# A decoder layer in float32: h's first quads in SP's queue, k tiles 8 and 9 by sevens in the tenth gate/up group, silu's product behind a split

## The chip, the cores and the metric

The kernel runs on one core of one Trainium2 chip. The metric is the device time of one launch in microseconds, the median of several runs. The core has TensorE (PE, with its weight loads as PEld), VectorE (DVE), ScalarE (ACT), GpSimd (POOL) and SyncE (SP). SP and POOL issue the DMAs here.

## What is computed

One decoder layer on 256 tokens of width 2048, in float32: a half-step SwiGLU FFN with LayerNorm, a token mixer (multi-head latent attention beside differential attention, merged by gates), a LayerNorm, and a second half-step FFN with LayerNorm. The change lies in the two FFNs:

```python
def _swiglu(x, w_gate, w_up, w_down):
    return (jax.nn.silu(x @ w_gate) * (x @ w_up)) @ w_down      # 2048 -> 5632 -> 2048

h = _layer_norm(ALPHA * h + 0.5 * _swiglu(h, ffn1_w_gate[l], ffn1_w_up[l], ffn1_w_down[l]), ln1_g[l], ln1_b[l])
mix = _mixer(h, ...)
h = _layer_norm(ALPHA * h + mix, ln2_g[l], ln2_b[l])
h = _layer_norm(ALPHA * h + 0.5 * _swiglu(h, ffn2_w_gate[l], ...), ln3_g[l], ln3_b[l])
```

## The kernel before

**Products.** A product in float32 is made of three matmuls (`triple`, L207 to L210): each operand is split into a high part of type fp32r and the rest, and high x high, high x low and low x high are summed in PSUM. So each weight block from memory is split first (`split`, L153 to L156): ScalarE casts it (the high part, L154), VectorE subtracts (the low part, L155). The two parts go into a ring of pairs of tiles (`wring`).

**Gate and up.** In `ffn`, the weights are taken in 22 chunks of 512 columns (256 of gate, 256 of up); the first two run by `project`, the other 20 by `Hybrid.group` (L374), in ten groups p = 1 to 10 of two chunks each, over all 16 k tiles of 128. A group treats some k tiles as 2 x 2 block products by seven multiplications in place of eight ("by sevens", with the sums of activations made once by `Seven` and `Extra`, and the sums of weight blocks made in each group on VectorE, L428, or by an accumulating DMA from POOL, L430). The rest is plain. With `wide` off, k tiles 0 to 7 go by sevens (14 seven-products of two k tiles) and 8 to 15 are plain (8 units). With `wide` on, k tiles 8 and 9 go by sevens too: a third slice of one k tile in each seven-product (`eraw`, 512 columns wide), 6 plain units, and one more element in each sum of weights. Groups 2 to 9 are wide, groups 1 and 10 are not. The order of the units is a string in `group` ("15pp6p72q4q3q" when wide: digits are seven-products, p and q plain units of the two chunks).

**Order of the work.** The units are issued with a look-ahead (`look(3, 4)`): 3 units are loaded ahead, 4 more are split ahead of the products. Small jobs are put in by `later(n, fn)`, n units on. The framework then schedules the instructions of each engine by a model of its own, so that an instruction without a reason to wait may be placed far ahead of where it was written. `tc.issue_after(x)` sets an instruction behind x on x's own engine. `behind_split(n)` sets one behind the n-th newest split of the weights. `fetched[0]` is the newest plain weight block's load (L457 in a group). Weight blocks are loaded from SP (L420 those of the sevens, L457 the plain ones).

**silu.** When a bank is complete, `sum_done` (L880) and `half` (L860) evacuate it (`gus`, L885), take silu on ScalarE (`sg`, L863) and multiply by the up part on VectorE (`hb`, L869; this is `product`). Two chunks make a tile of 512 columns, which `put_h` transposes by blocks (L715) and writes to `hT` in memory (L717).

**Down.** h comes back from `hT` in quads of 4 k tiles, in two halves of 128 tokens (256 KB each): `get_h` (L890) loads a quad from POOL (L893), `split_h` (L895) splits it (tiles `h`). The down product uses quads 3, 4 and 0 first; their loads are put in with the tenth group. Most activations and weights on the way share one pool of 41 tiles (tag `act`).

Of the kernel before, what the change touches and what calls it, by code (L numbers as in the profile page):

```python
# [11 lines left out]
F32 = mybir.dt.float32  # L12
# [3 lines left out]
ALU = mybir.AluOpType  # L16
AX = mybir.AxisListType

P = 128
# [4 lines left out]
KF = DFF // P  # L24
# [35 lines left out]
def layer_kernel(ctx: ExitStack, tc: tile.TileContext, a: dict, out: bass.AP):  # L60
    nc = tc.nc
    V, S, GP, PE = nc.vector, nc.scalar, nc.gpsimd, nc.tensor
# [9 lines left out]
    def nm(s):  # L72
        uid[0] += 1
        return f"{s}_{uid[0]}"

    def act_tile(shape, dt=F32, name="act"):
        return apool.tile(shape, dt, tag="act", name=nm(name), bufs=SLOTS)

    def tmp_tile(shape, name="tmp", dt=F32):
        return small.tile(shape, dt, tag="tmp", name=nm(name), bufs=6)  # L80
# [22 lines left out]
    def later(n, fn):  # L103
        uid[0] += 1
        heapq.heappush(todo, (step[0] + n, uid[0], fn))
# [45 lines left out]
    cast, lows, fetched = [None], [None], [None]  # L151
# [192 lines left out]
    def behind_split(n):  # L344
        return tc.issue_after(line[-n].ins) if len(line) >= n else nullcontext()
# [506 lines left out]
    def ffn(n, x, wgu, wdn, residual, g, bt, each, first=None, between=None, nxt=None, cols=None, norm=None, pending=None):  # L852
        hb = {}
        hT = dram.tile([KF // 4, 2, P, 512], F32, name=f"hT{n}")

        def put_h(b, q):
            with behind_split(1):
                turn_out(hb[b, q], hT[q, b])

        def half(c, b, up, gate, wait=0):  # L860
            q = c // 2
            sg = tmp_tile([P, 256], "sg")
            S.activation(sg, gate, AF.Silu)  # L863
            if c % 2 == 0:
                hb[b, q] = tmp_tile([P, 512], "hb")
            o = (c % 2) * 256

            def product():
                V.tensor_tensor(out=hb[b, q][:, o:o + 256], in0=up, in1=sg, op=ALU.mult)  # L869
            if wait:  # L870
                later(wait, product)
            else:
                product()
            if c % 2 == 1:
                later(12, lambda: put_h(b, q))
# [4 lines left out]
        def sum_done(c, b, bank, snap, op):  # L880
            if snap is None:
                gu_done(c, b, bank)
                return
            t = tmp_tile([P, 512], "gus")
            V.tensor_tensor(out=t, in0=bank, in1=snap, op=op)  # L885
            half(c, b, t[:, 256:512], t[:, 0:256], 1)

        got, hq = {}, {}

        def get_h(q):  # L890
            raw = got[q] = act_tile([P, 2, 512], F32, "hraw")
            for b in range(2):
                nc.gpsimd.dma_start(raw[:, b, :], hT[q, b])  # L893

        def split_h(q):  # L895
            raw = got.pop(q)
            hq[q] = [act_tile([P, 2, 4, P], F32R, "h") for _ in range(2)]
            for b in range(2):
                split(*(t[:, b].rearrange("p k (i c) -> p k i c", i=4) for t in hq[q]), turned(raw[:, b, :]))
# [31 lines left out]
        for p in range(1, KF // 4):  # L931
            if p == KF // 4 - 1:
                for i, q in enumerate((3, 4, 0)):
                    later(3 + 3 * i, lambda q=q: get_h(q))
                later(13, lambda: split_h(3))
                later(16, lambda: split_h(4))
            hy.group(wgu[2 * p], wgu[2 * p + 1],
                     lambda n, b, bank, snap, op, p=p: sum_done(2 * p + n, b, bank, snap, op),
                     1 < p < KF // 4 - 1, p > 1)
        ln = LayerNorm(0.5, residual, g, bt, each, nxt, cols,  # L940
                       ((24, 26, 48, 50) if pending is None else (13, 14, 60, 62), (94, 97, 100, 103)),
                       35 if cols is None else None, pending, () if pending is None else (17, 32, 67, 82))
# [10 lines left out]
        for p in range(2):  # L953
# [16 lines left out]
            for q in range(3, KF // 4):  # L970
                first_use = min(i for i, u in enumerate(units) if len(u) == 2 and u[1] // 2 == q)
                if q in kept or (p, q) in ((0, 3), (0, 4)):
                    continue
                call(first_use - 6, lambda q=q: get_h(q))
                call(first_use, lambda q=q: split_h(q))
            if p == 0:
                for q in range(3):
                    first_use = units.index((q, 1, None))
                    if q > 0:
                        call(first_use - 6, lambda q=q: get_h(q))  # L980
                    for i, fn in enumerate(forms[q].steps(lambda q=q: got[q])):
                        call(first_use + (0, 0, 1, 2, 3)[i], fn)
                    call(first_use + 3, lambda q=q: got.pop(q))
            else:
                call(len(units) - 8, widen)
            down.run(wdn[2 * p], wdn[2 * p + 1], units, forms,
                     lambda m, b, bank, sign, p=p: ln.fold(2 * p + m, b, bank, sign),
                     lambda m, b, bank, p=p: ln.evac(2 * p + m, b, bank), calls, 8 * p)
# [407 lines left out]

    h1 = Acts(KD, "h1", (0, 1))
    ffn(1, xq, a["gu1"], a["dn1"], a["x"], a["ln1_g"], a["ln1_b"], keep(0), first_tokens, second_tokens, h1, a["ln1_cols"])

    yq = mixer(h1)  # L1400
# [3 lines left out]
    for c in range(4):  # L1404
        project(a["w_out"][c], yq, KD, 512, lambda b, bank, c=c: ln.evac(c, b, bank),
                hook=at_unit(0, widen) if c == 3 else None)
    catch_up(0)

    ffn(2, h2, a["gu2"], a["dn2"], res[1], a["ln3_g"], a["ln3_b"],
        lambda b, c, z: nc.sync.dma_start(out[b * P:(b + 1) * P, c * 512:(c + 1) * 512], z), norm=ln,  # L1410
        pending=(a["ln2_g"], a["ln2_b"]))
# [85 lines left out]
```

## Time and profile before

| | us |
|---|---|
| median of 3 runs | 1973.62 (1973.51 to 1974.14) |
| the profiled execution | 1972.85 |
| its span, first to last instruction | 1971.1 |
| TensorE busy | 1955.1 |
| VectorE busy | 1773.5 |
| ScalarE busy | 1265.5 |
| first FFN, groups 2 to 10 | 92.5 to 455.3 |
| second FFN, groups 2 to 10 | 1366.4 to 1729.1 |

Busy time counts an engine's own instructions. Matmuls overlap in the pipeline, so a mean duration of 0.39 us of a matmul of 512 columns is not its share of the time: from start to start they follow each other faster. A wait is told by its row: "[1.91 <-ACT sg L863]" means that the engine sat idle for 1.91 us and that ScalarE's instruction of line 863 ended it.

### The profile page before, as it was taken

The page shows a single profiled execution, that of the slowest core. Times are in us where ns is not written, and L with a number is a line of the kernel's source. Part 1 is how long each engine was busy: PE and PEld are TensorE (multiplying, and loading weights), DVE is VectorE, ACT ScalarE, POOL GpSimd, SP SyncE. Part 2 cuts the span into 40 slices and gives each one's busy share as a digit, 9 for nine tenths or more (in the row PEclk, how much of TensorE's full clock was granted, in tenths as well). Part 3 has the DMA queues.
Part 4 walks back from the last instruction along what each step waited for, and adds up shares of the span by engine and source line. Part 5 has one row for each costly group of instructions (what it writes and reads, how often), then busy time and mean ns, then how long its engine had stood idle before and what let it go on. Part 6 is the DMA issues. An engine that isn't in the chain of part 4 may idle for free.

```text
span 1971.1 us, 25747 instructions
## 1 busy us (share of the span) xinstructions
PE 1955.1 (99%) x8784; PEld 1620.0 (82%) x8784; DVE 1773.5 (90%) x2175; ACT 1265.5 (64%) x1650; POOL 291.0 (15%) x503
## 2 busy tenths in 40 slices
PE   9999999999999999999999999999999999999997
PEld 7888888888888898888888888888888888888886
DVE  7999999999998879988976677789999999999986
ACT  6666767676655566666667765556676776665661
POOL 0112111122100010102223120001211112210000
PEclk9999999999999999999999999999999999999999
DMA  8978888777776666767667668578888878786763
GB/s 309 287 227 262 285 270 251 235 216 281 296 235 222 209 218 254 244 224 259 223 198 241 234 216 271 199 263 254 254 263 294 243 243 249 238 321 237 274 234 124
DMA packets 147478, 485.71 MB, mean 246 GB/s; under 512 B 20961, under 2 KB 21009, under 8 KB 147345
## 3 DMA queue, kind: packets, MB, share of 16 engines
q1 hardware_dynamic: 117360, 397.99, 58.2%
q0 software_dynamic: 29984, 86.07, 16.4%
q8 instruction: 69, 1.13, 0.2%
q14 instruction: 65, 0.52, 0.1%
HBM read 455.13 MB, written 28.84 MB: 246 GB/s over the span
## 4 chain that ended last, share of the span: by engine, by line
PE 95%; DVE 2%; DMA 1%; issue 1%; ACT 0%; SPq 0%; DVEq 0%; ACTq 0%
PE mm L209 30%; PE mm L210 30%; PE mm L208 30%; DVE wring L155 1%; PE tr L208 1%; PE tr L210 1%; PE tr L209 1%; DMA sraw<-in_gu_dram 1%; PE tr L671 0%; DVE sraw L428 0%; ACT wring L154 0%; DMA raw<-in_gu_dram 0%; PE tr L1228 0%; PE tr L1301 0%; PE tr L1303 0%
## 5 line engine op out<-in xcount | busy, mean ns | idle before, releaser
L154 ACT CAST wring<-raw 128x1024 fp32r<-128x1024 f32 (+2 forms) x467 | 482.2, 1038 | 296.5 <-PE mm L210 207.2
L155 DVE TENSOR_TENSOR wring<-raw,wring 128x1024 fp32r<-128x1024 f32 (+2 forms) x467 | 559.1, 1206 | 95.4 <-ACT wring L154 92.8
L154 ACT CAST wring<-sraw 128x1024 fp32r<-128x1024 f32 x436 | 454.8, 1054 | 230.2 <-DVE sraw L428 94.2
L155 DVE TENSOR_TENSOR wring<-sraw,wring 128x1024 fp32r<-128x1024 f32 x436 | 523.2, 1228 | 21.6 <-ACT wring L154 18.8
L210 PE MATMUL mm<-wring,h 128*128 128x512 f32 (+2 forms) x1248 | 480.2, 385 | 0.0
L208 PE MATMUL mm<-wring,h 128*128 128x512 f32 (+2 forms) x1248 | 480.2, 385 | 0.0
L209 PE MATMUL mm<-wring,h 128*128 128x512 f32 (+2 forms) x1248 | 479.8, 385 | 0.0
L209 PE MATMUL mm<-wring,xs 128*128 128x512 f32 x776 | 302.2, 389 | 1.3 <-DVE wring L155 1.3
L208 PE MATMUL mm<-wring,xs 128*128 128x512 f32 x776 | 302.2, 389 | 0.0
L210 PE MATMUL mm<-wring,xs 128*128 128x512 f32 x776 | 302.0, 389 | 0.0
L209 PEld LDWEIGHTS mm<-wring,h 128*128 128x128 f32 x1248 | 234.5, 188 | 46.8 <-DVE wring L155 0.7
L210 PEld LDWEIGHTS mm<-wring,h 128*128 128x128 f32 x1248 | 234.5, 188 | 46.5 <-DVE h L155 0.7
L208 PEld LDWEIGHTS mm<-wring,h 128*128 128x128 f32 x1248 | 234.4, 188 | 46.4 <-ACT h L154 0.6
L428 DVE TENSOR_TENSOR sraw<-sraw,sraw 128x1024 f32<-128x1024 f32 x168 | 200.2, 1229 | 3.5 <-DMA sraw<-in_wdv_dram 1.6
L209 PEld LDWEIGHTS mm<-wring,xs 128*128 128x128 f32 x776 | 145.7, 188 | 32.5 <-DVE wring L155 2.3
L208 PEld LDWEIGHTS mm<-wring,xs 128*128 128x128 f32 x776 | 145.7, 188 | 30.1
L210 PEld LDWEIGHTS mm<-wring,xs 128*128 128x128 f32 x776 | 145.7, 188 | 30.0
L717 POOL DMA_DIRECT2D hT<-blocks x176 | 97.1, 562 | 370.0 <-DVE blocks L715 368.2
L208 PE MATMUL mm<-wring,x 128*128 128x512 f32 x336 | 130.8, 390 | 0.8 <-ACT wring L154 0.8
L209 PE MATMUL mm<-wring,x 128*128 128x512 f32 x336 | 131.0, 390 | 0.5 <-DVE wring L155 0.5
L210 PE MATMUL mm<-wring,x 128*128 128x512 f32 x336 | 130.6, 389 | 0.0
L430 POOL DMA_DIRECT2D sraw<-in_gu_dram x40 | 35.6, 900 | 359.4 <-DVE sraw L428 309.0
(307 smaller groups left out, 2289.6 us busy)
## 6 DMA issues: line engine op xcount, KB each, us to landing
sraw<-in_gu_dram SPq DMA_DIRECT2D x160, 512.0 KB, 5.4
raw<-in_gu_dram SPq DMA_DIRECT2D x159, 512.0 KB, 4.7
raw<-in_dn_dram SPq DMA_DIRECT2D x140, 512.0 KB, 4.7
sraw<-in_gu_dram POOLq DMA_DIRECT2D x40, 512.0 KB, 6.9
sraw<-in_dn_dram SPq DMA_DIRECT2D x36, 512.0 KB, 5.6
hraw<-hT POOLq DMA_DIRECT2D x68, 256.0 KB, 6.2
eraw<-in_gu_dram SPq DMA_DIRECT2D x64, 256.0 KB, 6.0
raw<-in_w_out_dram SPq DMA_DIRECT2D x32, 512.0 KB, 4.3
```

Source lines behind the costliest of these rows:

```text
L154: cast[0] = S.copy(hi, src)
L155: lows[0] = V.tensor_tensor(out=lo, in0=src, in1=hi.bitcast(F32), op=ALU.subtract)
L208: PE.matmul(o, xh, wh, start=first, stop=False, skip_group_check=again)
L209: PE.matmul(o, xh, wl, start=False, stop=False, skip_group_check=again)
L210: PE.matmul(o, xl, wh, start=False, stop=last, skip_group_check=again)
L428: last = V.tensor_tensor(out=R[src][i], in0=R[src][i], in1=R[add[1]][i], op=ALU.add)
L430: nc.gpsimd.dma_start(R["12"][s], source("22", s), accum_op=ALU.add)
L717: nc.gpsimd.dma_start(to.rearrange("(g r) (i f) -> i r g f", g=4, i=4)[i], t[32 * i:32 * (i + 1), :].rearrange("r (g f) -> r g f", g=4))
```

## The change

Three edits, all in `ffn`. The product that was put off by one unit (`wait`) is issued on VectorE behind the third newest weight split. The loads of h's quads 3, 4 and 0, which the tenth group puts in, are made in halves from SP (`get_half`), each behind the newest plain weight block's load, at 1, 3, 5, 7, 9 and 11 units on; before, they came whole from POOL at 3, 6 and 9. `split_h` stays at 13 and 16. And the tenth group is wide too (`p > 1` in place of `1 < p < KF // 4 - 1`; KF // 4 is 11).

```diff
             def product():
-                V.tensor_tensor(out=hb[b, q][:, o:o + 256], in0=up, in1=sg, op=ALU.mult)
+                with behind_split(3) if wait else nullcontext():
+                    V.tensor_tensor(out=hb[b, q][:, o:o + 256], in0=up, in1=sg, op=ALU.mult)
...
+        def get_half(q, b):
+            if b == 0:
+                got[q] = act_tile([P, 2, 512], F32, "hraw")
+            with tc.issue_after(fetched[0].ins):
+                nc.sync.dma_start(got[q][:, b, :], hT[q, b])
...
         for p in range(1, KF // 4):
             if p == KF // 4 - 1:
                 for i, q in enumerate((3, 4, 0)):
-                    later(3 + 3 * i, lambda q=q: get_h(q))
+                    for b in range(2):
+                        later(1 + 4 * i + 2 * b, lambda q=q, b=b: get_half(q, b))
                 later(13, lambda: split_h(3))
                 later(16, lambda: split_h(4))
             hy.group(wgu[2 * p], wgu[2 * p + 1],
                      lambda n, b, bank, snap, op, p=p: sum_done(2 * p + n, b, bank, snap, op),
-                     1 < p < KF // 4 - 1, p > 1)
+                     p > 1, p > 1)
```

## The prediction

> **What bounds the kernel now.** I read the page first (busy times, then the chain that ended last), then who waited for whom on TensorE, then the busy times of single gate/up groups, and last the timelines around the two places where TensorE stood.
>
> ```profile
> PE 1955.1 (99%) x8784; PEld 1620.0 (82%) x8784; DVE 1773.5 (90%) x2175; ACT 1265.5 (64%) x1650; POOL 291.0 (15%) x503
> PE 95%; DVE 2%; DMA 1%; issue 1%; ACT 0%; SPq 0%; DVEq 0%; ACTq 0%
> PE mm L209 <- DVE wring L155: 1.8, 4, 0.7
> ```
>
> TensorE is busy for 99% of the span and is 95% of the chain. The third row (from the waits of TensorE over the whole span) says that its matmuls stood idle only 1.8 us in all for a split weight block. So there are two ways to gain: fewer matmuls, or one of these few waits. The groups, one row each (columns: stretch, length, then busy time and count for PE, PEld, DVE, ACT, POOL, granted clock, DMA share, GB/s):
>
> ```profile
> 334.23:374.35 40.12, 40.12 (x179) 33.23 (x177) 40.12 (x46) 27.87 (x36) 6.31 (x11) 1.00 0.84 256
> 374.35:414.47 40.12, 40.12 (x179) 33.23 (x177) 39.92 (x46) 28.37 (x37) 7.52 (x12) 1.00 0.77 234
> 414.47:455.27 40.80, 40.80 (x182) 33.80 (x180) 37.90 (x45) 26.67 (x33) 9.35 (x17) 1.00 0.71 217
> ```
>
> These are groups 8, 9 and 10 of the first FFN. Groups 8 and 9 are "wide" (k tiles 8 and 9 by sevens), the tenth is not: 177 weight loads against 180, and 40.12 us against 40.80. Both give the same pitch, 40.12 / 177 = 40.80 / 180 = 0.2267 us for each matmul, at a granted clock of 1.00: TensorE runs without a gap. But VectorE is full in a wide group, 40.12 of 40.12 us, and has 2.90 us to spare in the tenth. In these groups VectorE is the second bound, right behind TensorE.
>
> TensorE stands visibly at one place in each FFN's groups:
>
> ```profile
> 257.69 0.39 PE L208 MATMUL mm<-wring,xs 128*128 128x512 f32 x1
> 258.81 0.50 PE L209 MATMUL mm<-wring,xs 128*128 128x512 f32 x1 [0.73 <-DVE wring L155]
> 1531.68 0.39 PE L208 MATMUL mm<-wring,xs 128*128 128x512 f32 x1
> 1532.60 0.50 PE L209 MATMUL mm<-wring,xs 128*128 128x512 f32 x1 [0.53 <-DVE wring L155]
> ```
>
> From start to start that is 1.12 and 0.92 us instead of 0.2267, so 0.89 and 0.69 us are lost: 1.58 us. Why:
>
> ```profile
> 237.20 2.17 POOL L893 DMA_DIRECT2D hraw<-hT  x4 [2.13 <-DMA hT<-blocks]
> DMA  9599866987979989999999999999999999999999
> DMA packets 1282, 4.27 MB, mean 356 GB/s; under 512 B 179, under 2 KB 179, under 8 KB 1282
> 236.21 4.61 SPq L420 DMA_DIRECT2D sraw<-in_gu_dram  x4
> 247.38 1.05 ACT L154 CAST wring<-sraw 128x1024 fp32r<-128x1024 f32 x1 [2.71 <-DMA sraw<-in_gu_dram]
> 248.78 0.42 DVE L869 TENSOR_TENSOR hb<-gus,sg 128x256 f32<-128x256 f32 x1 [1.91 <-ACT sg L863]
> 1511.13 1.64 POOL L893 DMA_DIRECT2D hraw<-hT  x3 [1.38 <-DMA hT<-blocks]
> 1521.17 1.05 ACT L154 CAST wring<-sraw 128x1024 fp32r<-128x1024 f32 x1 [2.51 <-DMA sraw<-in_gu_dram]
> ```
>
> Four halves of h (`get_h`, L893; quads 4 and 0) leave POOL at 237.2, five groups before they are needed, beside the next group's weight blocks from SP. The two DMA rows cover 236 to 248: the DMA engines are full almost throughout. A block lands late, ScalarE's cast waits 2.71 us for it, the silu queued behind that cast is late, and VectorE, full anyway, stands 1.91 us at the product of L869. About ten microseconds later the lead of the splits is used up and TensorE stands. The second FFN repeats it (1511 to 1532).
>
> **The change part by part.**
>
> *Tenth group wide.* TensorE: 14 seven-products of 6 matmuls, 7 of 3 and 6 plain units of 12 are 177, where 14 x 6 + 8 x 12 were 180. Three matmuls fewer, 3 x 0.2267 = 0.68 us in each FFN, **-1.36 us**. VectorE pays for it:
>
> ```profile
> 249.12 2.35 DVE L155 TENSOR_TENSOR wring<-sraw,wring 128x1024 fp32r<-128x1024 f32 x2
> 251.39 0.68 DVE L155 TENSOR_TENSOR wring<-eraw,wring 128x512 fp32r<-128x512 f32 x1
> 252.00 2.35 DVE L428 TENSOR_TENSOR sraw<-sraw,sraw 128x1024 f32<-128x1024 f32 x2
> ```
>
> From start to start a split of 1024 takes (251.39 - 249.12) / 2 = 1.13 us and one of 512 takes 0.61; I take 0.61 for an add of 512 too. Seven more splits of 512, three more adds of 512 and two fewer splits of 1024: 4.27 + 1.83 - 2.26 = +3.84 us. So 37.90 + 3.84 = 41.7 us of VectorE's time meet 40.12 of TensorE's, 1.6 us too much. ScalarE gets seven casts of 512 for two of 1024, at most 5 x 1.05 = 5.3 us (1.05 is a cast of 1024, at 247.38), beside 40.80 - 26.67 = 14 us of idle time. The bytes of the weights stay the same but for one more accumulated slice of 256 KB on POOL.
>
> What covers the 1.6 us is the lead, the time from the end of a split to the matmul that reads it:
>
> ```profile
> 339.30 2.39 DVE L155 TENSOR_TENSOR wring<-raw,wring 128x1024 fp32r<-128x1024 f32 x2
> 341.25 0.39 PE L209 MATMUL mm<-wring,x 128*128 128x512 f32 x1
> 423.89 2.36 DVE L155 TENSOR_TENSOR wring<-sraw,wring 128x1024 fp32r<-128x1024 f32 x2
> 425.57 0.39 PE L209 MATMUL mm<-wring,xs 128*128 128x512 f32 x1
> 446.76 1.22 DVE L155 TENSOR_TENSOR wring<-raw,wring 128x1024 fp32r<-128x1024 f32 x1
> 452.55 0.39 PE L208 MATMUL mm<-wring,x 128*128 128x512 f32 x1
> ```
>
> In group 8 the seventh split ends at about 340.5 (the first of the two) and is read at 341.25: 0.7 us. In the tenth the narrowest place is 425.1 to 425.57, 0.45 us. At the tenth's end it is 452.55 - 447.98 = 4.6 us and more. So the 1.6 us can be paid out of the end; the danger is in the middle. There the four splits of quads 3 and 4 count:
>
> ```profile
> 384.29 0.74 DVE L155 TENSOR_TENSOR h<-hraw,h 128x512 fp32r<-128x512 f32 x1
> 395.83 0.74 DVE L155 TENSOR_TENSOR h<-hraw,h 128x512 fp32r<-128x512 f32 x1
> 423.29 0.69 DVE L155 TENSOR_TENSOR h<-hraw,h 128x512 fp32r<-128x512 f32 x1
> 431.84 0.69 DVE L155 TENSOR_TENSOR h<-hraw,h 128x512 fp32r<-128x512 f32 x1
> ```
>
> Two lie in group 9 and two in the tenth, 0.6 us of step each. Data that comes later moves one or both of the first into the tenth: what has to be covered there is 1.6 + 0.6 to 1.6 + 1.2 = 2.2 to 2.8 us.
>
> *h's halves in SP's queue.* Removed from POOL: six issues in each FFN. Added to SP: six, each behind the newest plain weight block (`fetched[0]`). I counted the units: 3 units are held loaded and 4 prepared, so the first three halves (both of quad 3, the first of quad 4) stand behind group 9's last plain block, the fourth behind the tenth's first, quad 0's two behind its second.
>
> ```profile
> 380.79 8.65 SPq L457 DMA_DIRECT2D raw<-in_gu_dram  x3
> 397.74 0.33 SPq L457 DMA_DIRECT2D raw<-in_gu_dram  x1
> 398.87 4.63 SPq L420 DMA_DIRECT2D sraw<-in_gu_dram  x4
> 406.88 1.05 ACT L154 CAST wring<-sraw 128x1024 fp32r<-128x1024 f32 x1 [0.68 <-DMA sraw<-in_gu_dram]
> ```
>
> The blocks are the second and third of the first row (about 381.6 and 389.1) and the one at 397.74. After 381.6 SP issues nothing for 7 us: three halves cost nothing there. Quad 0's two stand directly ahead of the four blocks at 398.87, and the tenth group's first product waits for those even now (0.68 us at 406.88). At the 356 GB/s of the burst above, 2 x 0.26 MB take 1.5 us, so that cast comes up to 1.5 us later. Behind it on ScalarE are silu and the next casts, behind those VectorE's splits, then TensorE. This is the old burst with two halves instead of four. The price lies between 0 (the tile of quad 0 is not free yet and the load is issued later, or the lead swallows it) and the old stall whole. I take half of the old stall, since half of the bytes are left: 1.58 goes, 0.79 comes, **-0.79 us**. If nothing comes it is -1.58.
>
> [...]
>
> *The product behind a split.* `behind_split(3)` adds an order on VectorE, no new data.
>
> ```profile
> 254.87 1.22 DVE L155 TENSOR_TENSOR wring<-sraw,wring 128x1024 fp32r<-128x1024 f32 x1
> 256.60 0.42 DVE L869 TENSOR_TENSOR hb<-gus,sg 128x256 f32<-128x256 f32 x1
> 258.67 0.42 DVE L869 TENSOR_TENSOR hb<-gus,sg 128x256 f32<-128x256 f32 x1
> ```
>
> When the last unit of a group is issued, four splits of the next have been traced; the third newest is the next group's second, 250.26 here. Both products stand behind its fourth (254.87) already. The product of the fourth form (248.78 above) stands behind the group's last split. So the order is kept today, and I cost the edit at nothing; behind the product wait only the transposes of hb and the writes of hT, which nobody needs soon. Bounds: one product moved past one split is 0.3 us either way at one place in a group, and TensorE sees it only where the lead is under 0.3, which is nowhere but at the two stalls.
>
> **The sum.** -1.36 - 0.79 = -2.15 us on the profiled execution's 1972.85 us (span 1971.1 and 1.75 around it): 1970.70. That execution lies 0.77 under the median of the runs, 1973.62, so the same step gives **1971.5 us**.
>
> **The rivals.**
>
> 1. *VectorE is overfull in the tenth group.* For it: 41.7 us of work in 40.12, up to 1.2 us of h splits on top, and a smallest lead of 0.45. Against it: 4.6 us of lead at the end, and groups 8 and 9 run wide without a gap. It decides if the h splits stand before the middle of the group, as at 423.29 now. At most 2.8 - 0.45 = 2.35 us is seen in each FFN: 1973.62 - 1.36 - 1.58 + 4.7 = **1975.4**, slower than before.
> 2. *The change doesn't relieve the DMA engines*, it moves the burst. The stall returns in full in the tenth group: 1973.62 - 1.36 = **1972.3**. For it: the full DMA row, and a cast that waits for its block already. Against: only two of six halves stand ahead of urgent blocks.
> 3. *SP is held.* An h load in SP's queue waits for a free tile of the 41, since the wide tenth group keeps its slices' tiles longer, and the weight blocks behind it come late. On POOL nobody urgent stood behind it. A block that was issued at 403 (the last of the row at 398.87) and comes 5 us late leaves VectorE idle for that; less the lead of 0.7, 4.3 us in each FFN: 1973.62 - 2.94 + 8.6 = **1979.3**. It decides once a load is held past the issue of such a block by more than 0.7. Against it: POOL got tiles for its four loads at 237, five groups early.
> 4. *The instructions are ordered anew elsewhere* and other waits shrink: TensorE's few waits leave little, 1969.5 or less.
>
> **How the numbers follow.** Chances: my forecast, 1970.4 to 1972, 0.50; rival 2, 0.17; rival 1, 0.15; rival 3, 0.12; rival 4, 0.06. A measurement of this kernel can tell about 0.2% from no change, that is 3.95 us, so faster means under 1969.7 and slower over 1977.6. Faster: rival 4, 0.06. Slower: rival 3, 0.12. The rest, 0.82, is within. The range from 1969.9 to 1976.2 takes in the forecast with both bounds and rivals 1 and 2, and leaves out rivals 3 and 4, 0.18.
>
> **What would show it.** Right: the tenth group takes 40.1 us with 177 matmuls; no POOL issue of hraw near 237 and 1511; no row of PE waiting for a split at 258 and 1532; the hraw loads on SP between 381 and 400; any new wait of PE near 420 to 430, under 0.5 us. Wrong: a PE wait of 1 us or more in the tenth group with VectorE busy throughout (rival 1) or with ScalarE waiting for a landing (rival 2); SP idle ahead of an hraw load with weight blocks behind it (rival 3); new waits of PE outside the gate/up groups (rival 4's kind, either sign).

## The result and the profile after

| | us |
|---|---|
| changed kernel, median of 17 runs | 1977.56 (1972.91 to 1979.94) |
| kernel before, median of 17 runs beside them | 1972.84 (1971.91 to 1975.28) |
| ratio | 1.0021, 95% interval 1.0014 to 1.0027 |
| the profiled execution of the changed kernel, its span | 1972.91, 1971.1 |

The change makes the kernel 0.21% slower: 4.1 us by the ratio, 4.7 by the medians. The forecast was 1971.5 us and "within 0.2%", in a range of 1969.9 to 1976.2; the median of 1977.56 lies outside it. The profiled execution is the shortest of the 17, so its trace shows the new waits at their smallest; two longer ones were profiled later (`after_look1`, `after_look2`). Below, "lost" time of TensorE is what its matmuls take from start to start beyond the pitch of 0.2267 us.

The page's busy times and its chain of the changed kernel, then (second fence) TensorE's waits over the span: us in total, times, longest.

```profile
PE 1954.2 (99%) x8778; PEld 1619.5 (82%) x8778; DVE 1780.2 (90%) x2191; ACT 1264.7 (64%) x1660; POOL 286.1 (15%) x493
PE 95%; DVE 3%; DMA 1%; ACT 1%; issue 0%; SPq 0%; DVEq 0%; ACTq 0%
```

```profile
PE tr L209 <- DVE wring L155: 1.7, 1, 1.7
PE mm L209 <- DVE wring L155: 1.5, 4, 0.5
```

Six matmuls fewer are there (8778 against 8784), and VectorE's share of the chain has grown from 2% to 3%. The first wait is new: a transposing matmul (`tr`) in the first FFN's down part. The tenth groups (columns as in the prediction):

```profile
412.52:453.47 40.95, 40.43 (x178) 33.15 (x177) 40.95 (x52) 29.77 (x40) 9.85 (x17) 1.00 0.68 194
1687.85:1728.80 40.95, 40.43 (x178) 33.15 (x177) 40.95 (x52) 29.11 (x39) 9.31 (x16) 1.00 0.67 195
```

177 weight loads as forecast, but 40.95 us, where 177 x 0.2267 is 40.13: 0.8 us are lost in each, and VectorE has no idle time at all. The loads of h, on SP's timeline, and the splits of quads 3 and 4, on VectorE's:

```profile
380.11 1.88 SPq L900 DMA_DIRECT2D hraw<-hT  x3
389.82 0.42 SPq L900 DMA_DIRECT2D hraw<-hT  x1
395.31 0.86 SPq L900 DMA_DIRECT2D hraw<-hT  x2
```

```profile
422.57 0.69 DVE L155 TENSOR_TENSOR h<-hraw,h 128x512 fp32r<-128x512 f32 x1
425.44 0.69 DVE L155 TENSOR_TENSOR h<-hraw,h 128x512 fp32r<-128x512 f32 x1
428.92 1.29 DVE L155 TENSOR_TENSOR h<-hraw,h 128x512 fp32r<-128x512 f32 x2
```

The six halves go out where the forecast put them, and no wait is left at 258 or 1532. All four splits of h now stand in the tenth group. And two of the three places where TensorE waits now (the third, at 1716.86 in the second FFN, repeats the first):

```profile
440.63 0.39 PE L208 MATMUL mm<-wring,xs 128*128 128x512 f32 x1
441.54 0.50 PE L209 MATMUL mm<-wring,xs 128*128 128x512 f32 x1 [0.52 <-DVE wring L155]
580.18 0.39 PE L208 MATMUL tr<-wring,xs 128*128 128x512 f32 x1
582.26 0.50 PE L209 MATMUL tr<-wring,xs 128*128 128x512 f32 x1 [1.69 <-DVE wring L155]
```

From start to start 0.91 and 2.08 us; with the matmul behind each, 0.79 and 1.96 are lost, and 0.79 at the third. In this execution the sum is about even: -1.36 for the matmuls, some -1.8 for the two old waits, +3.5 for the three new ones.

### The profile page after: what moved, and what is told of

Its sections match the earlier page's. It is cut to its first block, busy times and chain, and to the rows that moved or that the text cites. A ratio compares the mean times of both kernels' runs of the same rounds, so it can differ in the third digit from the quotient of the medians.

```text
span 1971.1 us, 25761 instructions
## 1 busy us (share of the span) xinstructions
PE 1954.2 (99%) x8778; PEld 1619.5 (82%) x8778; DVE 1780.2 (90%) x2191; ACT 1264.7 (64%) x1660; POOL 286.1 (15%) x493
## 4 chain that ended last, share of the span: by engine, by line
PE 95%; DVE 3%; DMA 1%; ACT 1%; issue 0%; SPq 0%; DVEq 0%; ACTq 0%
PE mm L209 30%; PE mm L210 30%; PE mm L208 30%; DVE wring L155 1%; PE tr L209 1%; PE tr L210 1%; PE tr L208 1%; PE tr L671 0%; ACT wring L154 0%; DMA raw<-in_gu_dram 0%; PE tr L1236 0%; PE tr L1309 0%; PE tr L1311 0%; DMA turned<-turn 0%; DMA raw<-in_dn_dram 0%
## 5 line engine op out<-in xcount | busy, mean ns | idle before, releaser
L155 DVE TENSOR_TENSOR wring<-raw,wring 128x1024 fp32r<-128x1024 f32 (+2 forms) x463 | 552.6, 1202 | 93.0 <-ACT wring L154 91.1
L209 PE MATMUL mm<-wring,x 128*128 128x512 f32 x330 | 128.6, 390 | 0.4 <-DVE wring L155 0.4
L208 PE MATMUL mm<-wring,x 128*128 128x512 f32 x330 | 128.4, 390 | 0.0
L210 PE MATMUL mm<-wring,x 128*128 128x512 f32 x330 | 128.3, 389 | 0.0
```

What stands on the lines that cost most here:

```text
L155: lows[0] = V.tensor_tensor(out=lo, in0=src, in1=hi.bitcast(F32), op=ALU.subtract)
L208: PE.matmul(o, xh, wh, start=first, stop=False, skip_group_check=again)
L209: PE.matmul(o, xh, wl, start=False, stop=False, skip_group_check=again)
L210: PE.matmul(o, xl, wh, start=False, stop=last, skip_group_check=again)
```

## The experiments

All ratios are to the kernel before, run beside the kernel on the same chip; a ratio is not the quotient of the two medians, and runs of different sets are not compared. "Lost" is in us, read from each kernel's one profiled execution.

| run | median us | ratio (95% interval) | lost in the tenth groups | lost at 500 to 600 | stretches at clock 0.5 there |
|---|---|---|---|---|---|
| after_again | 1975.62 | 1.0011 (1.0003 to 1.0020) | 0.78, 0.78 | 0.98 | 0 |
| only_sp | 1972.35 | 0.9998 (0.9989 to 1.0006) | 0, 0 | 0 | 0 |
| only_wide | 1979.58 | 1.0030 (1.0019 to 1.0042) | 0.78, 0.79 | 4.55 | 1 |
| wide_second | 1972.92 | 0.9997 (0.9988 to 1.0005) | 0, 0.79 | 0 | 0 |
| wide_first | 1977.27 | 1.0018 (1.0009 to 1.0027) | 0.78, 0 | 6.31 | 1 |
| after_look1 | 1978.01, one | | 1.05, 0.79 | 6.31 | 1 |
| after_look2 | 1977.56, one | | 0.79, 0.79 | 6.36 | 2 |
| setup_later | 1972.92 | 0.9998 (0.9989 to 1.0007) | 0.79, 0.79 | 0 | 0 |
| h_early | 1972.88 | 0.9999 (0.9990 to 1.0008) | 0.79, 0.79 | 2.95 | 0 |
| best_85 | 1976.17 | 1.0012 (1.0004 to 1.0021) | 0.79, 0.79 | 4.55 | 1 |
| best_20 | 1973.63 | 1.0002 (0.9993 to 1.0010) | 0.79, 0.79 | 2.19 | 0 |
| split_late | 1972.72 | 0.9997 (0.9988 to 1.0006) | 0.79, 0.79 | 0 | 0 |
| setup_held | 1971.75 | 0.9999 (0.9990 to 1.0007) | 0.79, 0.78 | 0 | 0 |
| q4_late | 1974.64 | 1.0007 (0.9998 to 1.0015) | 0, 0 | 3.24 | 0 |
| both_held | 1971.36 | 0.9993 (0.9984 to 1.0002) | 0, 0 | 0.26 | 0 |
| all_three | 1970.45 | 0.9989 (0.9980 to 0.9998) | 0, 0 | 0 | 0 |

### Which edit, and in which FFN

Two theories stood after the first trace. One: the overfull tenth group is the loss (the forecast's first rival). Two: the wide tenth group makes the framework order the instructions of the first FFN's down part anew, and the loss lies there, 130 us later. `after_again` is the change as it is; `only_sp` leaves the tenth group narrow, `only_wide` leaves h's loads whole on POOL; both leave out the third edit. That edit has no run of its own. `wide_second` has it and `only_sp` doesn't, and their first FFNs are otherwise the same: in their traces TensorE, VectorE, ScalarE and POOL take their instructions in the same order up to 860 us.

```diff
 only_sp (in place of the change's line)
-                     p > 1, p > 1)
+                     1 < p < KF // 4 - 1, p > 1)
 only_wide (in place of the change's lines)
-                    for b in range(2):
-                        later(1 + 4 * i + 2 * b, lambda q=q, b=b: get_half(q, b))
+                    later(3 + 3 * i, lambda q=q: get_h(q))
 wide_second                                wide_first
-  p > 1, p > 1)                           -  p > 1, p > 1)
+  1 < p < KF // 4 - (n == 1), p > 1)      +  1 < p < KF // 4 - (n == 2), p > 1)
```

> The changed kernel once more, since its runs lie between 1972.9 and 1979.9 us and the profiled one is the fastest of them. Theory 1 (the tenth group is overfull): in a run that is 4 to 6 us slower, TensorE's waits in the two tenth groups grow from the 0.8 us each of the first trace to 2 to 3 us each, and the first FFN's down part stays as it is. Theory 2 (the first FFN's down part): the tenth groups stay at about 0.8 us each, and the wait near 582 us, 1.96 us in the first trace, grows to 4 to 7 us, or new waits stand beside it between 500 and 660. Ratio to before under both: 1.001 to 1.003.

> Only h's halves go to SP's queue; the tenth group stays narrow and the product has no added order. Both theories: the two waits near 258 and 1532 us go and nothing comes in their place, so 1.2 to 1.8 us faster than before (ratio 0.9991 to 0.9994), and a small spread between runs. If the halves in SP's queue were what costs the time, it would be 2 us slower or more, with the spread of the changed kernel.

> Only the tenth group is wide in both FFNs; h is loaded from POOL as before. The waits near 258 and 1532 stay (1.6 to 1.8 us in all). Theory 1: two h splits lie in group 9 again, the tenth groups wait less than in the changed kernel, and the kernel is at most 2 us slower than before. Theory 2: the wide tenth group sets the order of the first FFN's down part anew whatever h does, so the loss and the spread of the changed kernel are there, 3 to 7 us slower than before.

> All three edits, but the tenth group is wide in the second FFN alone. Theory 1: half of the loss stays: about 2 us slower than before or as before. Theory 2: the first FFN is that of the halves alone, the second wide one costs only its 0.8 us, so 1.5 us faster than before (1.6 to 1.8 for the two waits that go, 0.7 for three matmuls, less 0.8), with a small spread.

> The changed kernel with the tenth group wide in the first FFN alone (the second FFN's tenth as before). Theory A (the wide tenth group of the first FFN makes the instructions of the first FFN's down part come in another order; VectorE's lead there runs out near 582 us): the whole loss stays, TensorE waits 1 to 3 us in all near 582 and 0.8 us near 442, nothing near 1717, and the median lies 2 to 5 us above the kernel before, ratio 1.001 to 1.0025. Theory B (the tenth group itself, overfull on VectorE, is the loss, the same in each FFN): a wait of 0.8 us at one place and half of the loss of the changed kernel, 1 to 2 us over the kernel with the second FFN's tenth wide alone or equal to it, ratio near 1.000.

The loss goes with the wide tenth group of the first FFN: `wide_first` and `only_wide` carry it, `only_sp` and `wide_second` do not. Yet the tenth groups of the two FFNs lose the same 0.79 us, so that group by itself is not the loss. The traces show the new order too: from 455 to 600 us TensorE and POOL take the same instructions in the same order in the kernel before and in the changed one, VectorE and ScalarE in another. From 460 to 600 us `only_wide` has the changed kernel's order on these two engines, so the wide group makes it. `after_again` itself decides little, since its profiled execution was again a short one (1972.17 us, 0.98 us lost at 582); its ratio, 1.0011 against 1.0021, says that the slowdown is 0.1 to 0.2%. The SP edit takes the two old waits away, as meant: `only_sp` has no wait in the gate/up groups, `only_wide` still loses 1.82 us near 258 and 0.69 near 1541. But neither `only_sp` nor `wide_second` is shown to be faster than the kernel before, where 1.2 to 1.8 and 1.5 us had been expected.

### What the two old waits were worth

> The kernel before once more, for its waits alone. If the waits of TensorE near 258 and 1532 us belong to the kernel and not to one execution, they stand here again with 0.5 us or more each, and no wait stands near 442, 582 or 1717. If they were chance, one or both are missing, and then the change had less to win than the 1.6 us of the forecast.

A second trace of the kernel before loses 0.40 us near 258 and 0.44 near 1536, not 1.0 and 0.8: a wait of such a size comes and goes with the execution. With the 2.51 of `only_wide`, there were 0.8 to 2.5 us to win, and the forecast's 1.58 was one reading of it. (This execution took 1976.28 us; its surplus lies in the mixer, which the change doesn't touch.)

### What a usual execution of the change looks like

> The changed kernel once more, for the trace of one more execution, since both traces of it so far are among its shortest executions. Theory A: the waits of VectorE's gaps and of the clock vary from one execution to the next. In an execution of 1976 us or more the surplus stands at 550 to 600 us (4 us or more of lost time there, against 1.96 in the trace of 1972.91), with a stretch of 3.4 us at a clock of 0.5 behind it. Rival C: the surplus stands elsewhere (in the mixer, 900 to 1150 us, or spread evenly), and the waits at 550 to 600 stay at 1 to 2 us.

> The same again, as one execution may be a short one: theory A, 4 us or more lost at 550 to 600 us with a stretch at clock 0.5 if the execution takes 1976 us or more, 1 to 2 us lost there and no such stretch if it takes under 1973; rival C, the surplus elsewhere.

Both fell on long executions, 1978.01 and 1977.56 us, and both bear out theory two. One row for 545 to 600 us from each trace (weight loads are the second count): the kernel before, the changed kernel's profiled execution, and `after_look1`.

```profile
545.00:600.00 55.00, 55.00 (x245) 45.54 (x244) 54.41 (x88) 34.13 (x38) 3.75 (x7) 1.00 0.75 243
```

```profile
545.00:600.00 55.00, 53.31 (x235) 43.83 (x235) 52.84 (x85) 34.03 (x40) 3.75 (x7) 1.00 0.71 235
```

```profile
545.00:600.00 55.00, 51.74 (x215) 40.94 (x214) 52.15 (x81) 31.40 (x37) 4.88 (x10) 0.97 0.74 239
```

In the same 55 us TensorE takes 244, 235 and 214 weights: 9 x 0.2267 = 2.0 us lost in the short execution, 30 x 0.2267 = 6.8 in the long one (6.3 in the table, by its longer gaps alone). Part of that is no wait but clock. TensorE's rows of `after_look1`, then two stretches of 3.41 us (the last three columns are the granted clock, the DMA share and GB/s):

```profile
582.30 0.39 PE L210 MATMUL mm<-wring,h 128*128 128x512 f32 x1
583.28 0.50 PE L208 MATMUL tr<-wring,xs 128*128 128x512 f32 x1 [0.60 <-ACT wring L154]
585.61 0.50 PE L209 MATMUL tr<-wring,xs 128*128 128x512 f32 x1 [1.82 <-DVE wring L155]
...
587.85 0.63 PE L210 MATMUL mm<-wring,h 128*128 128x512 f32 x1
588.28 0.63 PE L208 MATMUL mm<-wring,h 128*128 128x512 f32 x1
```

```profile
583.30:586.71 3.41, 1.59 (x6) 1.10 (x7) 3.41 (x4) 2.77 (x3) 0.00 (x0) 1.00 0.64 191
586.71:590.12 3.41, 3.41 (x10) 2.67 (x9) 3.41 (x5) 1.05 (x1) 0.00 (x0) 0.50 0.80 253
```

Two waits (0.98 and 2.33 us from start to start) are followed by 3.41 us at a clock of 0.50, in which matmuls start 0.43 us apart instead of 0.2267: 3.41 x (1 - 0.2267 / 0.43) = 1.6 us lost. By that, one such stretch takes 3.41 x 0.50 / 1976 = 0.0009 off the mean clock of the span. 13 of the changed kernel's first 17 runs have a mean of 0.997 or less, but only 4 of the 11 of `after_again`; of the kernel before it is 2 of 30, 5 of 27, 6 of 23, 2 of 33 and 2 of 15 in the five sets beside the experiments. The mean doesn't say where a stretch lies: the profiled executions of `wide_second`, `split_late` and `both_held` have a mean of 0.997 too, and no stretch at clock 0.5 at 500 to 600 us. The account of this execution against the profiled one of before, 5.1 us longer in span: -1.36 matmuls, -1.8 old waits, +1.84 tenth groups, +6.31 here makes +5.0.

### Why VectorE's lead runs out

Take the weight block whose first matmul starts near 560 us, 72 matmuls ahead of the down part's transposes. In the kernel before, VectorE ends its split 4.45 us ahead of that matmul; in the changed kernel, 1.29 us (561.41 - 556.96, and 559.78 - 558.49).

```profile
555.74 1.22 DVE L155 TENSOR_TENSOR wring<-raw,wring 128x1024 fp32r<-128x1024 f32 x1
...
561.41 0.39 PE L208 MATMUL mm<-wring,h 128*128 128x512 f32 x1
```

```profile
557.27 1.22 DVE L155 TENSOR_TENSOR wring<-raw,wring 128x1024 fp32r<-128x1024 f32 x1
...
559.78 0.39 PE L208 MATMUL mm<-wring,h 128*128 128x512 f32 x1
```

The lead goes in three gaps of VectorE (1.92 us at 535 and the two below), and these go back to loads of h. From the timeline of the changed kernel, POOL, ScalarE and VectorE:

```profile
531.70 0.62 ACT L154 CAST h<-hraw 128x512 fp32r<-128x512 f32 x1 [2.03 <-DMA hraw<-hT]
...
540.19 2.12 POOL L894 DMA_DIRECT2D hraw<-hT  x4 [11.96 <-ACT wring L154]
...
543.91 0.62 ACT L154 CAST h<-hraw 128x512 fp32r<-128x512 f32 x1 [3.87 <-DMA hraw<-hT]
...
545.51 1.23 DVE L155 TENSOR_TENSOR wring<-sraw,wring 128x1024 fp32r<-128x1024 f32 x1 [1.71 <-ACT wring L154]
...
548.25 1.23 DVE L155 TENSOR_TENSOR wring<-raw,wring 128x1024 fp32r<-128x1024 f32 x1 [1.52 <-ACT wring L154]
```

And the same loads and casts in the kernel before:

```profile
530.33 0.62 ACT L154 CAST h<-hraw 128x512 fp32r<-128x512 f32 x1 [0.82 <-DMA hraw<-hT]
...
534.06 1.07 POOL L893 DMA_DIRECT2D hraw<-hT  x2 [7.33 <-DVE h L155]
```

Before, POOL's third pair of loads leaves at 534.06; in the new order its tile comes free only at 540.19, released by a weight cast of ScalarE. ScalarE reaches the cast of h first and sits 3.87 us in front of it, and the weight casts come only behind; VectorE has nothing to split. Behind the dip, from 551.7, come the instructions of `setup` (mask, biases and angles for the mixer, put in 70 units after the tenth group) and LayerNorm's, so that VectorE has no room to win the lead back. In the second FFN there is no `setup`, and no wait.

How much lead is needed can be read from all traces together. The matmul that waits at 582.26 is the 91st behind the one at 559.78, and reads the eleventh split behind. Wherever `setup` stands in this stretch, the lead shrinks by 3.1 us from the one to the other, or TensorE waits for what is missing (us, by the traces' unrounded times; the 0.11 us behind the waiting matmul is not in):

| trace | lead near 560 | lost up to the waiting matmul | lead there |
|---|---|---|---|
| before | 4.46 | 0 | 1.36 |
| only_sp | 4.59 | 0 | 1.49 |
| split_late | 4.35 | 0 | 1.25 |
| after_again | 2.28 | 0.87 | 0.05 |
| after | 1.30 | 1.85 | 0.05 |
| h_early | 0.21 | 2.94 | 0.06 |
| q4_late | -0.01 | 3.16 | 0.05 |
| after_look2 | -0.30 | 3.45 | 0.05 |
| after_look1 | -0.88 | 4.03 | 0.05 |

With `setup` out of the stretch it shrinks by 1.96 us only: from 2.60 to 0.64 in `setup_held`, from 4.75 to 2.79 in `all_three`. So the four traces of the changed kernel differ here by the lead that VectorE brings along, and the wait follows from it.

Each link was undone in a run of its own (`lows[0]` is the newest split's VectorE instruction):

```diff
 setup_later        -            later(70, setup)
                    +            later(100, setup)
 h_early (in h's loads of the first FFN's first pass)
-                call(first_use - 6, lambda q=q: get_h(q))
+                call(first_use - (10 if n == 1 and p == 0 else 6), lambda q=q: get_h(q))
 split_late (the same loop; the split of h)
-                call(first_use, lambda q=q: split_h(q))
+                call(first_use + (2 if n == 1 and p == 0 else 0), lambda q=q: split_h(q))
 setup_held         -            later(70, setup)
                    +            later(80, setup_held)
+    def setup_held():
+        with tc.issue_after(lows[0].ins):
+            setup()
```

> The changed kernel with the preparation of mask, biases and angles (setup) put in 100 units after the tenth group instead of 70. Theory A says that the wait near 582 us needs two things, a lead of 1.5 us at the end of the down part's first pass and the instructions of setup on VectorE right behind it: with setup some 25 us later the wait at 582 goes or falls under 0.4 us, the waits of 0.8 us near 442 and 1717 stay, and the median falls by 1 to 3 us against the changed kernel, ratio to the kernel before 0.999 to 1.0005. Rival (the lead is gone without setup): the wait near 582 stays at 1 us or more. A further way to miss: setup's work collides with what comes 25 us later, and a wait of the same size appears after 600.

> The changed kernel with the loads of h's later quads in the first FFN's first down pass put in ten units ahead of their use instead of six. Theory A says that ScalarE's casts of h wait for late landings there (1 to 4 us at 532 to 546 us) and that this takes VectorE's lead: if the earlier loads land earlier, ScalarE waits under 0.5 us there, the lead at the end of the pass is back above 3 us, the wait near 582 goes, and the ratio to the kernel before is 0.999 to 1.0003. Rival (the loads wait on POOL for a free tile, 11 to 12 us, whenever they are issued): the landings and the wait near 582 stay as they are, ratio 1.001 to 1.002.

> The changed kernel with the splits of h's later quads in the first FFN's first down pass two units later; loads, setup and all else as in the change. Theory A (casts of h that wait for their landing hold ScalarE's weight casts): ScalarE's waits for landings at 531 to 548 us fall from 1 to 5 us to under 1, VectorE's gaps there to under 1, the lead at the end of the pass stays above 3 us, and the waits near 582 and the stretch at clock 0.5 behind them go; median 1972 to 1973.5, ratio 0.9990 to 1.0003. Rival (the new order itself puts too much on VectorE there): gaps small but the wait near 582 stays, ratio 1.001 or more.

> The changed kernel with setup tied on VectorE behind the split that is newest at 80 units, so that its instructions really run later (some 60 places later on VectorE, about 600 to 640 us). Theory A: VectorE's gaps at 531 to 548 stay, but the waits near 582 fall under 0.5 us in all, no stretch at clock 0.5 follows there, and the wait of 1.8 us at 686 that setup at 100 units brought doesn't come; median 1971.5 to 1973, ratio 0.9990 to 1.0000. Rival (the lead is gone without setup): waits of 1 us or more near 582, ratio 1.001 or more.

`setup_held` keeps the gaps: VectorE waits 6.0 us for weight casts at 528 to 550, three times, the longest 3.1. But its lead at the place above is 2.59 us (559.93 - 557.34), enough for the 1.96 that the stretch takes without `setup`, and no wait follows.

```profile
556.12 1.22 DVE L155 TENSOR_TENSOR wring<-raw,wring 128x1024 fp32r<-128x1024 f32 x1
...
559.93 0.39 PE L208 MATMUL mm<-wring,h 128*128 128x512 f32 x1
```

`split_late` keeps `setup` and makes the gaps smaller: VectorE is idle for 2.6 us at 528 to 550, where it is 5.2 in the changed kernel and 1.6 in the kernel before. Its waits of ScalarE, then of VectorE, at 528 to 550:

```profile
ACT h L154 <- DMA hraw<-hT: 4.0, 1, 4.0
```

```profile
DVE h L155 <- ACT h L154: 3.4, 1, 3.4
DVE wring L155 <- ACT wring L154: 1.5, 2, 1.2
```

ScalarE still waits 4.0 us for one landing, against what was expected. But weight casts now stand ahead of it, so of VectorE's waits for weight casts only 1.5 us are left, the lead at the same place is 4.35 us (559.83 - 555.48, from the rows of that split and matmul), and TensorE doesn't wait there. So either remedy took the wait away, the later casts of h or the later `setup`. Neither run undoes one link alone: in `split_late` the order on VectorE and ScalarE is a third one, and POOL's third pair of loads left at 534.43 again, and in `setup_held` the lead near 560 rose too. And it is a matter of amounts: `both_held` holds `setup` back as well, came to the place with a lead of 1.86, and lost 0.26 us.

`h_early` missed, as its rival said: POOL's third pair of loads left at 540.40 us, four units earlier in the program and no earlier on the chip, since it waits for a tile; the wait near 582 stayed, 2.95 us lost. Its median is nevertheless level with the kernel before. Its one trace has no stretch at clock 0.5 at 500 to 600 us, and 3 of its 11 runs have a mean clock of 0.997 or less, much as the 4 of 11 of `after_again`. More tiles than 41 weren't tried. `setup_later` removed the wait at 582 and lost 1.95 us at 686 instead of 0.29, where LayerNorm's last VectorE work came late behind `setup`.

### The tenth group, and a version without the waits

```diff
 best_85, best_20   -                later(16, lambda: split_h(4))
                    +                later(22, lambda: split_h(4))
                    -            later(70, setup)
                    +            later(85, setup)        (best_20: 20)
 q4_late            -                later(16, lambda: split_h(4))
+                def split_4():
+                    with behind_split(1):
+                        split_h(4)
+                later(28, split_4)
 both_held = setup_held + q4_late;  all_three = both_held + split_late
```

> The changed kernel with two moves: setup at 85 units after the tenth group (between the 70 of the change and the 100 of the run before, where TensorE waited 1.8 us at 686 for VectorE), and the split of quad 4 six units later (22 instead of 16), out of the tenth group's narrow stretch. Theory A: no wait near 582 nor near 686 over 0.5 us; the two splits of quad 4 run after 441 us, so the waits of 0.8 us near 442 and 1717 fall to under 0.3; median 1970.5 to 1972.5, ratio 0.9985 to 0.9998. Rival: VectorE's surplus in the tenth group is not paid by the later split, and the 0.8 us stays; ratio 0.9995 to 1.0005.

> The same with setup at 20 units, ahead of the dip of VectorE's lead (where the lead is 5 to 9 us) in place of behind it. Theory A: the lead after the dip is lower by what setup takes of VectorE's time there and has not won back, so a wait near 545 to 585 of 0 to 2 us; if the lead of 5 to 9 us is enough, no wait over 0.5 us in the first FFN's down part at all, and none near 686; ratio 0.9985 to 1.0000. If setup's work delays the h splits, ratio over 1.001.

> The changed kernel with the split of quad 4 behind the tenth group's narrow stretch (at 28 units, tied behind the newest weight split: four weight splits later on VectorE than at step 22). Theory (the tenth group is overfull on VectorE where these two splits of 0.6 us stand): no wait over 0.3 us at 442 or 1717, where 0.8 us stood in every run of the wide tenth group; the waits near 582 stay as in the change, median 1975 to 1978. Rival: VectorE is overfull without them, and 0.4 us or more of the wait stays.

> setup tied later and quad 4's split late, both together: the change with its two waits taken away. Theory: no wait over 0.5 us in either FFN; what is left against the kernel before is six matmuls fewer (1.36 us) and the waits at 258 and 1532 (0.8 to 1.6 us): median 1970.5 to 1972, ratio 0.9985 to 0.9995. If VectorE's surplus only moves on, a new wait of 0.5 us or more stands in the first 40 us of the down part and the ratio is 0.9995 to 1.001.

> The change with quad 4's split behind the narrow stretch, setup tied later and the casts of h in the first FFN's first down pass two units later. Theory: VectorE's gaps at 531 to 548 us under 1.2 us as in split_late, the lead in the down part above 3 us, no wait over 0.3 us in either FFN, no stretch at clock 0.5 in the FFNs. Median 1970.5 to 1972, 1 to 2.5 us under the kernel before, ratio 0.9985 to 0.9996, no better than both_held since that has no wait left either. Rival (each undoing shifts the order again): a new wait over 0.5 us somewhere in the down part and a median of 1972.5 or more.

`best_85` missed on both counts: `setup` at 85 units still ran at 553 us, since nothing ties it, and the splits of quad 4 moved but stayed ahead of the narrow place. `best_20` ran `setup` at 483 to 510 us and moved the wait to 508 to 513. In `q4_late` the two splits stand behind the narrow place (first fence, VectorE), and TensorE's pitch is unbroken where 0.91 us stood between these two matmuls before (second fence):

```profile
446.46 1.28 DVE L155 TENSOR_TENSOR h<-hraw,h 128x512 fp32r<-128x512 f32 x2
```

```profile
441.47 0.39 PE L208 MATMUL mm<-wring,xs 128*128 128x512 f32 x1
441.70 0.39 PE L209 MATMUL mm<-wring,xs 128*128 128x512 f32 x1
```

The waits near 582 stayed in `q4_late`, as expected. With nearly all waits taken away the wide tenth group seems to pay. `both_held` is 2.0 us under the kernel before by the medians, not settled by its interval. `all_three` is 2.07 us under it, ratio 0.9989 (0.9980 to 0.9998), about what six matmuls (1.36) and the old waits (0.8 to 2.5) are worth, less the 0.91 us that it still loses at 473; that new wait is the one of its rival, though the median isn't. Of the table's fourteen ratios it is the only one whose interval lies under 1, and that narrowly, so one more set of runs would be needed to rely on it.

## Why the prediction was wrong, point by point

- **Six matmuls fewer, -1.36.** Right: 8778 matmuls, 177 in each tenth group.
- **h's halves on SP, -0.79.** The halves left where they were counted, no half held SP (rival 3 did not come), and nothing of the stall came back in the groups (`only_sp`: no wait there; rival 2 did not come). The term was mis-sized: its whole is -0.8 to -2.5 by execution, and the half that was to come back never came.
- **The product behind a split, 0.** Right: no instruction moved.
- **The tenth group.** Rival 1's mechanism, at a third of its price and in addition to the forecast: 0.79 us in each FFN against "at most 2.35". It stands at 441, not at 420 to 430: the leads at the four h splits held, and the debt came due 12 us later, ahead of the lead at the group's end. Of the 2.2 to 2.8 us that the working had to cover, the leads ahead of 441 covered all but 0.79; the 4.6 us at the end, from which it was to be paid, come behind. `q4_late` shows that quad 4's two splits make the difference.
- **The step that failed:** the change's cost was looked for in the gate/up groups, on SP and on POOL, and everything behind the tenth group was taken to stay as it was. "The instructions are ordered anew elsewhere" stood as rival 4 with 0.06, and only as a gain, because TensorE's few waits left little to lose in the trace of before. But waits that are there bound what a new order can gain, not what it can cost; what it can cost hangs on the leads. VectorE was busy for 54.41 of 55 us at 545 to 600 before. Its lead there was 4.45 us, of which the stretch takes 3.1; in the four traces of the change it came with 2.28 to -0.88. This lost 0.98 to 6.36 us, in the two longer executions with stretches of 3.41 us at a clock of 0.50 in it (one and two); without the loss (`setup_held`, `split_late`) the change is level with the kernel before. The last sentence of the forecast named the sign of it, new waits outside the gate/up groups, without a price.

Shown by runs: that the loss comes with the first FFN's wide tenth group and lies in its down part, that the wait there follows from VectorE's lead and goes when the lead is restored or `setup` is held back, and that quad 4's splits make the tenth group's wait. Argued from the traces alone: that the casts of h which hold ScalarE are what takes the lead, and why the tile comes free later in the new order (a release by ScalarE's weight cast in place of VectorE's split of h).

## What to carry to other kernels

Where a scheduler places the instructions, price an edit over the whole stretch in which the order can change, by the leads there and by what stands behind them on the same engines, not by the waits that the old trace shows. Before an engine is given an instruction that waits for a landing, look at what stands behind it in that engine's order (here ScalarE sat 3.87 us in front of a cast of h, with weight casts behind it) and whether the tile for the load can come free without that work. A small change of a long kernel is read from several profiled executions: the one trace here was the shortest of 17, and its sum was even.

## What the hardware showed

In `after_look1` TensorE's clock stood at 0.50 for 3.41 us, from 586.71 on. In the 3.41 us ahead, at a clock of 1.00, 2.2 us of TensorE's time had been lost (2.10 from 583.28 to 585.61, 0.10 behind it), and it was busy for 1.59 us. In `after_look2` the clock stood at 0.50 for twice as long, from 583.67 to 590.49; in the 3.42 us ahead, at 1.00, TensorE was busy for 1.65. Here are two stretches of 3.41 us from each of two more executions with the waits near 582, `h_early`, then `wide_first`.

```profile
581.55:584.96 3.41, 1.62 (x7) 1.37 (x8) 3.41 (x4) 2.25 (x3) 0.00 (x0) 1.00 0.82 227
584.96:588.38 3.42, 3.42 (x17) 2.81 (x16) 3.42 (x6) 1.58 (x2) 0.81 (x2) 1.00 0.85 258
```

```profile
582.39:585.80 3.41, 1.01 (x4) 0.35 (x3) 3.41 (x4) 3.41 (x4) 0.00 (x0) 1.00 0.46 151
585.80:589.22 3.42, 3.42 (x9) 2.65 (x10) 3.42 (x5) 0.42 (x2) 0.00 (x0) 0.50 0.90 232
```

The waits are the same in both, 0.6 and 1.8 us of idle time. In `h_early` TensorE is busy for 1.62 us of the first stretch, and the clock stays at 1.00; in `wide_first` for 1.01, and the next stretch runs at 0.50. The changed kernel's profiled execution has 1.72 of 3.41 us busy at 579.79 to 583.20, with 1.96 lost, and the clock stays at 1.00 in the 3.42 us behind. In `q4_late` 1.96 and 2.42 of 3.41 us are busy, at 579.18 to 582.59 and 582.59 to 586.00, at a clock of 1.00 in both. What decides it is not shown by these six executions: 1.65 us busy came ahead of the low clock, 1.62 did not. So the same waits were followed by 3.41 us at the low clock in one execution, 1.6 us lost by the working above, and by none in another, which can be part of why the runs of the changed kernel spread over 7 us.
